# Strassen's scheme for the feed-forward up projection of a two-layer encoder

## The chip, the cores and the metric

The kernel runs on one core of a Trainium2 chip. The metric is the device time of one execution in microseconds (us); less is better. TensorE (PE in the profile) multiplies matrices, VectorE (DVE), ScalarE (ACT) and GpSimd (POOL) do element-wise work, and SyncE (SP) issues the transfers.

## The reference

Two layers over 512 tokens of 1024 features, in float32. The part that the change touches is the end of each layer:

```python
x = x + merged @ w_out[l]                       # 512x1024 @ 1024x1024
h = rms_norm(x, norm_ffn[l])                    # x * rsqrt(mean(x*x) + eps) * g
x = x + jnp.square(jax.nn.relu(h @ w_ff1[l])) @ w_ff2[l]   # 1024x4096, 4096x1024
```

Ahead of it each layer projects `x`, runs three kinds of attention, and sums their gated branches into `merged`; none of that is changed.

## The kernel before

Everything is feature-major: a tile is 128 features by 512 tokens, so `x` is eight tiles `x[0..7]`, and a result tile of a projection is one PSUM bank. For precision every operand is split into a high part that TensorE takes as it is and the rest: weights into `whi` (a copy on ACT, L140) and `wlo = raw - whi` (a subtraction on DVE, L142), inputs likewise. A product is three matmuls, `whi*xgh`, `whi*xgl` and `wlo*xgh` (`feature_tile`, L326, matmul at L333). `Stream.take` (L127) loads 512 KB of weights (eight 128x128 blocks) into one of three `raw` buffers and splits them.

`merge` (L907) ends with the output projection: eight tiles of 8 x 3 matmuls over 512 tokens. As each ends, DVE adds it to `x[m]` (L935) and `norm_part` (L264) makes the feed-forward's input: `xgh` on ACT (L273), `xgl` on DVE (L274), the square of `x[m]` on ACT (L284), added into `acc` on POOL (L285). The input is not yet divided by the root mean square: that factor, one per token, is found meanwhile and multiplied on afterwards.

`ffn` (L946) follows. **Up**: 32 tiles `up(f)` of 8 x 3 matmuls over 512 tokens; the first four are interleaved so that `norm_sums` (L296: eight small matmuls `ps_sum` over `acc`, then a chain on DVE) and `norm_rows` (L317: the factor spread to all partitions, `rb`) fall between them. What leaves PSUM is `max(ps, 0) * rb` (DVE, L957), its square split into `ah` (ACT) and `al` (DVE, L961 and L962). **Down**: after every 16 up tiles, eight tiles over the 16 new features, each added to `x[m]` by DVE (L991).

TensorE runs its matmuls in the order in which they are written. The queues of the other engines are ordered by a scheduler: what a `high_priority` block encloses (all of a weight's load and split) is taken ahead of its place, by `ahead` = 30 steps. An engine works its queue strictly in order. Buffers: `raw`, `whi`, `wlo` three each, `xgh` and `xgl` eight each; PSUM banks `mm` three, `s` two, `pt` two, `y` one.

## Time and profile before

| | |
|---|---|
| median of 3 runs | 1852.36 us (1851.02 to 1852.7) |
| profiled execution, its own time | 1852.28 us |
| its span in the profile | 1850.4 us |
| granted TensorE clock over the span | 0.993 |
| busy share: PE, DVE, ACT, POOL | 98%, 54%, 42%, 18% |

The span runs from the first to the last recorded instruction; the time has 1.9 us around it. A duration is that of one instruction by itself; instructions in a queue overlap a little, so the distance from start to start in a row of them is shorter.

### The profile page before, as it was taken

What the parts mean: (1) busy time and instruction counts of PE and PEld (TensorE: products, weight loads), DVE (VectorE), ACT (ScalarE), POOL (GpSimd) and SP (SyncE); (2) the same over time, 40 slices, a digit from 0 to 9 for tenths busy, and PEclk for the clock granted to TensorE, in tenths of its full rate; (3) what the DMA queues carried; (4) which work ended last, traced back from release to release, by engine and by line L of the source; (5) the groups of instructions that cost most, each with busy time, mean ns of one, the idle gap of its engine ahead of it and who ended that gap; (6) DMA issues with size and microseconds to landing.
All of it is one profiled execution on the core that took longest, in us unless ns stands there. A gap on an engine that the chain in (4) does not pass through costs nothing.

```text
span 1850.4 us, 23224 instructions
## 1 busy us (share of the span) xinstructions
PE 1811.2 (98%) x8496; PEld 1492.8 (81%) x8496; DVE 995.2 (54%) x1894; ACT 783.1 (42%) x1369; POOL 332.6 (18%) x307
## 2 busy tenths in 40 slices
...
GB/s 180 153 168 115 102 177 153 117 97 81 114 171 91 94 100 91 95 99 109 115 118 149 154 110 112 176 149 120 84 89 135 150 91 92 102 92 93 101 114 57
DMA packets 84225, 217.84 MB, mean 118 GB/s; under 512 B 13696, under 2 KB 16768, under 8 KB 84112
## 3 DMA queue, kind: packets, MB, share of 16 engines
...
## 4 chain that ended last, share of the span: by engine, by line
PE 85%; DVE 6%; ACT 3%; DMA 2%; issue 2%; POOL 1%; SPq 1%; ACTq 0%; DVEq 0%; POOLq 0%
PE ps L333 38%; PE ps_t L368 15%; PE ps_f L333 14%; PE ps_o L333 5%; PE ps_b L803 4%; PE ps_s L683 3%; PE ps_y L726 3%; PE ps_p L713 2%; DMA qq<-nat 1%; PE ps_q L585 1%; POOL wlo L142 1%; SPq L600 1%; DVE wlo L142 1%; ACT whi L140 1%; DVE pr L692 0%
## 5 line engine op out<-in xcount | busy, mean ns | idle before, releaser
L140 ACT ACTIVATE whi<-raw 128x1024 fp32r<-128x1024 f32 (+1 forms) x337 | 307.4, 919 | 772.0 <-issue 318.1
L142 DVE TENSOR_TENSOR wlo<-raw,whi 128x1024 fp32r<-128x1024 f32 (+2 forms) x237 | 287.1, 1212 | 233.7 <-ACT whi L140 233.1
L333 PE MATMUL ps<-ah,wlo 128*128 128x512 f32 x512 | 201.7, 394 | 0.0
L333 PE MATMUL ps<-ah,whi 128*128 128x512 f32 x512 | 201.7, 394 | 0.0
L333 PE MATMUL ps<-al,whi 128*128 128x512 f32 x512 | 201.7, 394 | 0.0
L333 PE MATMUL ps<-xgh,whi 128*128 128x512 f32 x512 | 199.4, 390 | 0.0
L333 PE MATMUL ps<-xgh,wlo 128*128 128x512 f32 x512 | 199.2, 389 | 0.0
L333 PE MATMUL ps<-xgl,whi 128*128 128x512 f32 x512 | 199.2, 389 | 0.0
L333 PE MATMUL ps_f<-xgh,whi 128*128 128x512 f32 x464 | 197.2, 425 | 0.0
L333 PE MATMUL ps_f<-xgl,whi 128*128 128x512 f32 x464 | 183.3, 395 | 0.0
L333 PE MATMUL ps_f<-xgh,wlo 128*128 128x512 f32 x464 | 183.2, 395 | 0.0
L142 POOL TENSOR_TENSOR wlo<-raw,whi 128x1024 fp32r<-128x1024 f32 x50 | 120.8, 2416 | 222.2 <-ACT whi L140 178.2
L368 PE MATMUL ps_t<-whi,xgh 128*128 128x512 f32 x384 | 151.4, 394 | 6.8 <-ACT whi L140 6.8
L368 PE MATMUL ps_t<-wlo,xgh 128*128 128x512 f32 x384 | 150.2, 391 | 0.0
L368 PE MATMUL ps_t<-whi,xgl 128*128 128x512 f32 x384 | 150.2, 391 | 0.0
L285 POOL TENSOR_TENSOR acc<-acc,t 128x512 f32<-128x512 f32 x24 | 41.5, 1730 | 499.1 <-ACT t L284 489.7
L716 DVE TENSOR_TENSOR ptl<-ps_p,pth 128x512 fp32r<-128x512 f32 x144 | 85.8, 600 | 67.8 <-ACT pth L715 66.9
L333 PEld LDWEIGHTS ps<-ah,wlo 128*128 128x128 f32 x512 | 95.7, 187 | 23.8
L333 PEld LDWEIGHTS ps<-ah,whi 128*128 128x128 f32 x512 | 95.7, 187 | 23.8
L333 PEld LDWEIGHTS ps<-al,whi 128*128 128x128 f32 x512 | 95.7, 187 | 23.5
L333 PEld LDWEIGHTS ps<-xgh,wlo 128*128 128x128 f32 x512 | 96.1, 188 | 20.2
L333 PEld LDWEIGHTS ps<-xgl,whi 128*128 128x128 f32 x512 | 96.1, 188 | 19.9
...
## 6 DMA issues: line engine op xcount, KB each, us to landing
...
```

Of the source, the lines that this page charges most:

```text
L140: nc.scalar.activation(out=hi[:, c : c + v], in_=raw[:, c : c + v], func=AF.Copy)
L142: k.lo_engine.tensor_tensor(out=lo[:, c : c + w], in0=raw[:, c : c + w], in1=hi[:, c : c + w].bitcast(F32), op=ALU.subtract)
L285: (engine or nc.gpsimd).tensor_tensor(out=self.acc, in0=self.acc, in1=sq, op=ALU.add)
L333: nc.tensor.matmul(out=ps, lhsT=a[:, k], rhs=b[k], start=first and k == 0 and j == 0, stop=last and k == n - 1 and j == 2)
L368: nc.tensor.matmul(out=pss[t][:, 0:width], lhsT=a[k][:, t * P : t * P + P], rhs=b[:, i], start=c == 0 and i == 0 and j == 0, stop=last and ...
L585: nc.tensor.transpose(ps[0:rows, t * P : (t + 1) * P], src(t), self.ident)
L600: nc.sync.dma_start(out=s[rows, u].bitcast(F32), in_=x[own].bitcast(F32))
L683: nc.tensor.matmul(out=ps[:, 0:n], lhsT=a[:, i * P : (i + 1) * P], rhs=b[:, 0:n], start=j == 0, stop=j == len(terms) - 1)
L713: nc.tensor.transpose(ps[:, o + (i - kb) * P : o + (i - kb + 1) * P], pr[:, offs[i] + kb * P : offs[i] + (kb + 1) * P], self.ident)
L716: nc.vector.tensor_tensor(out=pl[:, 0:w], in0=ps[:, 0:w], in1=ph[:, 0:w].bitcast(F32), op=ALU.subtract)
L726: nc.tensor.matmul(out=yps[:, kb * P : T], lhsT=qkv[2][kb // 2][:, kb % 2, h, :], rhs=head[h][gi][x][:, o : o + T - kb * P], start=gi == 0 ...
L803: nc.tensor.matmul(out=pss[u], lhsT=chunk[a][:, u, k], rhs=y[b][k], start=k == 0 and j == 0, stop=k == 3 and j == 2)
```

## The change

A pair of up tiles (256 features by 512 tokens, 1024 deep) is computed as 2x2 blocks by Strassen's scheme in Winograd's form: seven products of half depth, half features and half tokens in place of eight. Of the inputs (halves of the depth times halves of the tokens) and of the weights, four sums or differences each enter beside the plain blocks, and the seven results are summed into the four blocks of the pair.

- Weights (`Stream.take_pair`): two loads of 512 KB, four subtractions of 512 columns on POOL (`tw`), and four splits instead of two: `bh`/`bl` (512 columns), `whi`/`wlo`, and twice `twh`/`twl` (1024 each); two buffers each for `bh`, `bl`, `tw`, `twh`, `twl`.
- Inputs (`norm_pair`, in the place of `norm_split`): the tiles `x[m]` and `x[m + 4]` together give the seven factors as `xgh`/`xgl` and `sh`/`sl`. It is called as the output projection's tiles end, whose order is now 0, 4, 1, 5, 2, 6, 3, 7. `sh` and `sl` lie in a pool on the side on which the last branch's buffers were.
- Products (`pair_products`): 16 pairs of 7 x 4 x 3 = 84 matmuls over 256 tokens, in four PSUM banks, alternately `y, mm, mm, mm` and `s, s, pt, pt`. The first pair runs depth block by depth block, the others product by product.
- Sums (`pair_sum`): a copy of 256 columns on ACT, then four additions on DVE into `z` (one buffer), the later of them reading what the earlier wrote. Relu, square and `ah` follow on ACT over 1024 columns, `al` on DVE. The factor `rb` no longer multiplies here.
- `down` runs after every four pairs, over 8 features' tiles at a time; its result is multiplied by `rb*rb` on DVE and then added to `x[m]`, two instructions for one.
- `norm_sums` is written behind pair 1 and `norm_rows` behind pair 2.

The new layout of `w_ff1` (blocks of a pair side by side) is left out of this diff.

```diff
@@ class Stream @@
+    def take_pair(self, pool, *key):
+        k, nc = self.k, self.k.nc
+        raw = [k.pw.tile([P, 1024], F32, tag="raw", name="raw") for _ in range(2)]
+        sums = [pool.tile([P, 1024], F32, tag="tw", name="tw", bufs=2) for _ in range(2)]
+        w = {}
+        def split(names, src, n, tags):
+            hi, lo = (p.tile([P, n], F32R, tag=t, name=t, **b) for p, t, b in tags)
+            nc.scalar.activation(out=hi[:, 0:n], in_=src[:, 0:n], func=AF.Copy)
+            nc.vector.tensor_tensor(out=lo[:, 0:n], in0=src[:, 0:n], in1=hi[:, 0:n].bitcast(F32), op=ALU.subtract)
+            for i, name in enumerate(names):
+                w[name] = tuple(x[:, 512 * i : 512 * i + 512].rearrange("p (k m) -> p k m", m=P) for x in (hi, lo))
+        with k.tc.high_priority(k.ahead):
+            for i in range(2):
+                nc.sync.dma_start(out=raw[i], in_=self.ap[self.layer, :, self.at + 1024 * i : self.at + 1024 * i + 1024])
+            b = [raw[i][:, 512 * j : 512 * j + 512] for i in range(2) for j in range(2)]
+            t = [sums[i][:, 512 * j : 512 * j + 512] for i in range(2) for j in range(2)]
+            sub = lambda out, x, y: nc.gpsimd.tensor_tensor(out=out, in0=x, in1=y, op=ALU.subtract)
+            plain = ((k.pw, "whi", {}), (k.pw, "wlo", {}))
+            summed = ((pool, "twh", dict(bufs=2)), (pool, "twl", dict(bufs=2)))
+            split(["b11"], raw[0], 512, ((pool, "bh", dict(bufs=2)), (pool, "bl", dict(bufs=2))))
+            split(["b21", "b22"], raw[1], 1024, plain)
+            sub(t[0], b[1], b[0])
+            sub(t[1], b[3], t[0])
+            split(["t1", "t2"], sums[0], 1024, summed)
+            sub(t[2], b[3], b[1])
+            sub(t[3], b[2], t[1])
+            split(["t3", "t4"], sums[1], 1024, summed)
...
@@ class Kern @@
+    def norm_pair(self, l, vcol, pool, kt, x):
+        nc = self.nc
+        h2 = T // 2
+        a, b = slice(0, h2), slice(h2, T)
+        g = self.gain(l, vcol + kt)
+        if kt < 4:
+            self.half = self.half if kt else {}
+            t = self.half[kt] = self.tmp()
+            nc.scalar.activation(out=t, in_=x, func=AF.Copy, scale=g)
+            return
+        t = self.half.pop(kt - 4)
+        q = pool.tile([P, 3, h2], F32, tag="sq", name="sq", bufs=1)
+        sub = lambda out, u, v: nc.vector.tensor_tensor(out=out, in0=u, in1=v, op=ALU.subtract)
+        h = self.px.tile([P, T], F32R, tag="xgh", name="xgh")
+        lo = self.px.tile([P, T], F32R, tag="xgl", name="xgl")
+        nc.scalar.activation(out=h, in_=x, func=AF.Copy, scale=g)
+        sub(q[:, 1], t[:, a], t[:, b])
+        nc.vector.scalar_tensor_tensor(out=t[:, b], in0=x[:, b], scalar=g, in1=t[:, b], op0=ALU.mult, op1=ALU.add)
+        sub(q[:, 0], t[:, b], t[:, a])
+        nc.vector.scalar_tensor_tensor(out=q[:, 2], in0=x[:, a], scalar=g, in1=q[:, 0], op0=ALU.mult, op1=ALU.subtract)
+        nc.vector.scalar_tensor_tensor(out=lo, in0=x, scalar=g, in1=h.bitcast(F32), op0=ALU.mult, op1=ALU.subtract)
+        f = {"a12": [y[:, a] for y in (h, lo)], "a22": [y[:, b] for y in (h, lo)]}
+        h = self.px.tile([P, T], F32R, tag="xgh", name="xgh")
+        lo = self.px.tile([P, T], F32R, tag="xgl", name="xgl")
+        nc.scalar.activation(out=h, in_=t, func=AF.Copy)
+        sub(lo, t, h.bitcast(F32))
+        f |= {"a11": [y[:, a] for y in (h, lo)], "s1": [y[:, b] for y in (h, lo)]}
+        h = pool.tile([P, 3, h2], F32R, tag="sh", name="sh", bufs=4)
+        lo = pool.tile([P, 3, h2], F32R, tag="sl", name="sl", bufs=4)
+        nc.scalar.activation(out=h, in_=q, func=AF.Copy)
+        sub(lo, q, h.bitcast(F32))
+        for i in range(3):
+            f[f"s{2 + i}"] = [y[:, i] for y in (h, lo)]
+        self.xf.append(f)
...
-    def norm_rows(self):
-        nc = self.nc
-        ps = self.pt.tile([P, T], F32, tag="pt", name="ps_r")
+    def norm_rows(self, tag=None):
+        nc = self.nc
+        ps = self.bank(tag, "ps_r") if tag else self.pt.tile([P, T], F32, tag="pt", name="ps_r")
...
@@ merge @@
-                self.norm_part(l, V_FFN, m, x[m])
-            outs = [out(m) for m in range(KT)]
+                self.norm_pair(l, V_FFN, pool, m, x[m])
+                self.norm_square(m, x[m])
+            self.xf = []
+            outs = [out(m) for m in (0, 4, 1, 5, 2, 6, 3, 7)]
...
+    PRODUCTS = (
+        ("b11", "a11", 0, 0),
+        ("b21", "a12", 1, 0),
+        ("t2", "s2", 1, 1),
+        ("t3", "s3", 2, 0),
+        ("t1", "s1", 2, 1),
+        ("t4", "a22", 3, 0),
+        ("b22", "s4", 3, 1),
+    )
+    def pair_products(self, w, tags, steps):
+        nc = self.nc
+        h2 = T // 2
+        ps = [None] * 4
+        n = len(self.xf)
+        for i, k in steps:
+            stationary, moving, bank, half = self.PRODUCTS[i]
+            if ps[bank] is None:
+                ps[bank] = self.bank(tags[bank], f"ps_w{bank}")
+            out = ps[bank][:, half * h2 : half * h2 + h2]
+            hi, lo = w[stationary]
+            xh, xl = self.xf[k][moving]
+            for j, (a, b) in enumerate(((hi, xh), (hi, xl), (lo, xh))):
+                nc.tensor.matmul(out=out, lhsT=a[:, k], rhs=b, start=k == 0 and j == 0 and i in (0, 1, 3, 5), stop=k == n - 1 and j == 2 and i in (0, 2, 4, 6))
+            yield
+        self.ps = ps
+    def pair_sum(self, ps, z):
+        nc = self.nc
+        h2 = T // 2
+        add = lambda out, x, y: nc.vector.tensor_tensor(out=out, in0=x, in1=y, op=ALU.add)
+        two = lambda x: x.rearrange("p (u t) -> p u t", u=2)
+        p1 = self.tmp()[:, 0:h2]
+        nc.scalar.activation(out=p1, in_=ps[0][:, 0:h2], func=AF.Copy)
+        add(z[:, 0:5:4], two(ps[1]), p1.unsqueeze(1).to_broadcast([P, 2, h2]))
+        add(z[:, 5:7], two(ps[2]), z[:, 4].unsqueeze(1).to_broadcast([P, 2, h2]))
+        add(z[:, 3], ps[2][:, h2:T], z[:, 5])
+        add(z[:, 1:3], two(ps[3]), z[:, 5:7])
+        return z[:, 0:4].rearrange("p (u v) t -> p u (v t)", u=2)
...
@@ ffn @@
-            pa = self.pool(ctx, "act", 16)
-            xg = self.nx
-            def up(f, out):
-                hi, lo = self.streams[l].take(1024, "f1", f)
-                ps = self.bank("s" if f == 3 else "mm", "ps_1")
-                yield from self.feature_tile(ps, [c.rearrange("p (k m) -> p k m", m=P) for c in (hi, lo)], *xg)
+            pf = self.pool(ctx, "ffn", 1)
+            pa = self.pool(ctx, "act", 4)
+            take = lambda j: self.streams[l].take_pair(pf, "f1", j)
+            def up(j, w, a):
+                steps = [(i, k) for k in range(4) for i in range(7)] if j == 0 else [(i, k) for i in range(7) for k in range(4)]
+                yield from self.pair_products(w, (("y", "mm", "mm", "mm"), ("s", "s", "pt", "pt"))[j % 2], steps)
+                c = self.pair_sum(self.ps, pf.tile([P, 7, T // 2], F32, tag="z", name="z"))
+                nc.scalar.activation(out=c, in_=c, func=AF.Relu)
+                nc.scalar.activation(out=c, in_=c, func=AF.Square)
+                h, lo = pa.tile([P, 2, T], F32R, tag="ah", name="ah"), pa.tile([P, 2, T], F32R, tag="al", name="al")
+                nc.scalar.activation(out=h, in_=c, func=AF.Copy)
+                nc.vector.tensor_tensor(out=lo, in0=c, in1=h.bitcast(F32), op=ALU.subtract)
+                for u in range(2):
+                    a[0].append(h[:, u])
+                    a[1].append(lo[:, u])
+            def down(q, m, a):
+                ps = self.mm.tile([P, T], F32, tag="mm", name="ps_2")
+                w = self.streams[l].take(1024, "f2", 8 * q, m)
+                yield from self.feature_tile(ps, [c.rearrange("p (k m) -> p k m", m=P) for c in w], *a)
                 t = self.tmp()
-                nc.vector.scalar_tensor_tensor(out=t, in0=ps, scalar=0.0, in1=self.rb, op0=ALU.max, op1=ALU.mult)
-                h = pa.tile([P, T], F32R, tag="ah", name="ah")
-                lo = pa.tile([P, T], F32R, tag="al", name="al")
-                nc.scalar.activation(out=h, in_=t, func=AF.Square)
-                nc.vector.tensor_tensor(out=t, in0=t, in1=t, op=ALU.mult)
-                nc.vector.tensor_tensor(out=lo, in0=t, in1=h.bitcast(F32), op=ALU.subtract)
-                out[0].append(h)
-                out[1].append(lo)
-            for half in range(2):
+                nc.vector.tensor_tensor(out=t, in0=ps, in1=rb2, op=ALU.mult)
+                nc.vector.tensor_tensor(out=x[m], in0=x[m], in1=t, op=ALU.add)
+                if q == 3:
+                    if l + 1 < DEPTH:
+                        nc.sync.dma_start(out=self.xd[:, m], in_=x[m])
+                        self.norm_part(l + 1, V_MIX, m, x[m])
+                    else:
+                        nc.sync.dma_start(out=self.a["out"][:, m], in_=x[m])
+            w = take(0)
+            for q in range(4):
                 a = ([], [])
-                ups = [up(16 * half + f, a) for f in range(16)]
-                if half == 0:
-                    for u in ups[0:2]:
-                        for _ in range(7):
-                            next(u)
-                    self.norm_sums()
-                    next(ups[0])
-                    next(ups[1])
-                    for _ in range(7):
-                        next(ups[2])
-                    self.norm_rows()
-                    next(ups[2])
-                    for _ in range(7):
-                        next(ups[3])
-                for u in ups:
-                    run_all(u)
-                if half == 1 and l + 1 < DEPTH:
+                for j in range(4 * q, 4 * q + 4):
+                    ahead = take(j + 1) if j % 4 < 3 else None
+                    run_all(up(j, w, a))
+                    w = ahead
+                    if j == 1:
+                        self.norm_sums()
+                    if j == 2:
+                        self.norm_rows("mm")
+                        rb2 = self.rb
+                        nc.vector.tensor_tensor(out=rb2, in0=rb2, in1=rb2, op=ALU.mult)
+                if q == 3 and l + 1 < DEPTH:
                     self.norm_begin()
-                for m in range(KT):
-                    ps = self.mm.tile([P, T], F32, tag="mm", name="ps_2")
-                    for c in range(2):
-                        hi, lo = self.streams[l].take(1024, "f2", 16 * half + 8 * c, m)
-                        run_all(self.feature_tile(ps, [w.rearrange("p (k m) -> p k m", m=P) for w in (hi, lo)], a[0][8 * c : 8 * c + 8], a[1][8 * c : 8 * c + 8], first=c == 0, last=c == 1))
-                    nc.vector.tensor_tensor(out=x[m], in0=x[m], in1=ps, op=ALU.add)
-                    if half == 1:
-                        if l + 1 < DEPTH:
-                            nc.sync.dma_start(out=self.xd[:, m], in_=x[m])
-                            self.norm_part(l + 1, V_MIX, m, x[m])
-                        else:
-                            nc.sync.dma_start(out=self.a["out"][:, m], in_=x[m])
+                downs = [down(q, m, a) for m in range(KT)]
+                for d in downs[0:2]:
+                    for _ in range(6):
+                        next(d)
+                for i, d in enumerate(downs):
+                    if i == 5 and q < 3:
+                        w = take(4 * q + 4)
+                    run_all(d)
...
@@ run @@
-                self.merge(l, y, x)
+                ps = self.pool(xctx, "sums", 1, side="right")
+                self.merge(l, y, x, ps)
```

On DVE, at the end of the output projection (`ps_o` are its results; `x_5224` is the last tile of `x`, `nv` reads the sums of squares), before:

```order
L935 TENSOR_TENSOR x_5224<-x_5224,ps_o 128x512
L142 TENSOR_TENSOR wlo<-raw,whi 128x1024
L274 SCALAR_TENSOR_TENSOR xgl<-x_5224,vec,xgh 128x512
L304 TENSOR_SCALAR nv<-ps_sum 128x4
```

and now (`t_5729` is the scaled `x[3]`, `sq` the three sums of inputs):

```order
L1008 TENSOR_TENSOR x_5224<-x_5224,ps_o 128x512
L139 TENSOR_TENSOR bl<-raw,bh 128x512 x2
L333 SCALAR_TENSOR_TENSOR t_5729<-x_5224,vec,t_5729 128x256
L336 SCALAR_TENSOR_TENSOR xgl<-x_5224,vec,xgh 128x512
L139 TENSOR_TENSOR twl<-tw,twh 128x1024 x2
L328 TENSOR_TENSOR sq<-t_5729 128x256
L328 TENSOR_TENSOR xgl<-t_5729,xgh 128x512
L139 TENSOR_TENSOR wlo<-raw,whi 128x1024
L335 SCALAR_TENSOR_TENSOR sq<-x_5224,vec,sq 128x256
L328 TENSOR_TENSOR sl<-sq,sh 128x768
```

The rests `bl` and `twl` of the first pair's weights stand behind the last addition of the output projection, and the last input factors `sl` behind them and behind a `wlo` of the second pair.

On DVE, from the first pair's sums (`ps_w_58..` are its PSUM banks, `ps_w_5986` to `ps_w_6036` those of the second pair) to the reader of the sums of squares, now:

```order
L1055 TENSOR_TENSOR z<-ps_w_5864,z 128x512
L139 TENSOR_TENSOR bl<-raw,bh 128x512
L1082 TENSOR_TENSOR al<-z,ah 128x1024
L139 TENSOR_TENSOR wlo<-raw,whi 128x1024
L139 TENSOR_TENSOR twl<-tw,twh 128x1024 x2
L1055 TENSOR_TENSOR z<-ps_w_5986,t_6062 128x2x256
L178 TENSOR_TENSOR wlo<-raw,whi 128x1024
L1055 TENSOR_TENSOR z<-ps_w_6011,z 128x512
L1055 TENSOR_TENSOR z<-ps_w_6011,z 128x256
L1055 TENSOR_TENSOR z<-ps_w_6036,z 128x512
L377 TENSOR_SCALAR nv<-ps_sum 128x4
```

The matmuls `ps_sum` take the PSUM bank `ps_w_6011`, so they wait for its last reader, `z<-ps_w_6011,z 128x256`. A `wlo` of pair 3's weights, the two `twl` of pair 2's and a `wlo` of the down projection now stand ahead of it in the queue (pairs are counted from 0).

On POOL, at the end of the output projection (`t_57..` are squares of `x[m]`), before:

```order
L285 TENSOR_TENSOR acc<-acc,t_5658 128x512
L285 TENSOR_TENSOR acc<-acc,t_5697 128x512
L285 TENSOR_TENSOR acc<-acc,t_5736 128x512
L285 TENSOR_TENSOR acc<-acc,t_7632 128x512
```

and now:

```order
L358 TENSOR_TENSOR acc<-acc,t_5694 128x512
L358 TENSOR_TENSOR acc<-acc,t_5731 128x512
L148 TENSOR_TENSOR tw<-raw 128x512 x2
L148 TENSOR_TENSOR tw<-raw,tw 128x512 x2
L148 TENSOR_TENSOR tw<-raw 128x512
L148 TENSOR_TENSOR tw<-raw,tw 128x512
L358 TENSOR_TENSOR acc<-acc,t_5783 128x512
L148 TENSOR_TENSOR tw<-raw 128x512
L148 TENSOR_TENSOR tw<-raw,tw 128x512
```

The four subtractions for pair 0 stand behind the `acc` of the seventh tile in the output projection's order (`t_5731`, of `x[3]`), followed by two of pair 1's; only then comes the last `acc`.

## Rows read from the trace of the kernel before

**Rows 1.** The page's busy line: busy us, share of the span, instructions.
```profile
PE 1811.2 (98%) x8496; PEld 1492.8 (81%) x8496; DVE 995.2 (54%) x1894; ACT 783.1 (42%) x1369; POOL 332.6 (18%) x307
```

**Rows 2.** The page's chain that ended last, shares of the span by engine.
```profile
PE 85%; DVE 6%; ACT 3%; DMA 2%; issue 2%; POOL 1%; SPq 1%; ACTq 0%; DVEq 0%; POOLq 0%
```

**Rows 3.** The chain's pieces at layer 0's up projection: start, length, what.
```profile
571.42 9.55 PE ps L333 x42
580.97 0.79 PE ps_sum L293 x8
...
588.61 337.69 PE ps L333 x1467
```

**Rows 4.** Windows, output projection and half up: PE, PEld, DVE, ACT, POOL busy, clock, DMA, GB/s.
```profile
526.62:571.42 44.80, 44.80 (x194) 36.10 (x193) 23.19 (x28) 17.55 (x25) 10.31 (x6) 1.00 0.33 98
571.42:749.00 177.58, 177.58 (x777) 144.57 (x776) 79.91 (x111) 43.88 (x51) 1.79 (x1) 1.00 0.32 95
```

**Rows 5.** Timeline of PE, attention of layer 0: start, us, instruction.
```profile
446.27 0.28 PE L726 MATMUL ps_y<-pth,v 128*128 128x256 f32 x1
446.39 0.28 PE L726 MATMUL ps_y<-ptl,v 128*128 128x256 f32 x1
```

**Rows 6.** The same view, earlier.
```profile
423.36 0.52 PE L683 MATMUL ps_s<-st 96*128 96x256 f32 x3
423.71 0.60 PE L585 MATMUL ps_q<-ident,tok 128*96 128x128 f32 x4
424.07 0.48 PE L333 MATMUL ps_f<-xgh,whi 128*128 128x512 f32 x1
```

**Rows 7.** Groups of DVE by form: busy us, mean ns; idle before.
```profile
L142 DVE TENSOR_TENSOR wlo<-raw,whi 128x1024 fp32r<-128x1024 f32 x227 | 279.7, 1232 | 226.6 <-ACT whi L140 225.9 <-DMA t<-rows 0.5
...
L991 DVE TENSOR_TENSOR x<-x,ps 128x512 f32<-128x512 f32 x32 | 22.0, 688 | 119.0 <-PE ps L333 119.0
L716 DVE TENSOR_TENSOR ptl<-ps_p,pth 128x256 fp32r<-128x256 f32 x48 | 20.3, 422 | 30.4 <-ACT pth L715 29.7
```

**Rows 8.** Groups of ACT by form.
```profile
L140 ACT ACTIVATE whi<-raw 128x1024 fp32r<-128x1024 f32 x227 | 240.4, 1061 | 725.8 <-issue 315.5 <-PE ps L333 246.7 <-PE ps_t L368 96.0
L140 ACT ACTIVATE whi<-raw 128x512 fp32r<-128x512 f32 x102 | 61.5, 621 | 25.1 <-PE ps_t L368 20.4 <-issue 2.7 <-PE ps_f L333 2.1
```

**Rows 9.** Timeline of POOL, two additions of one form.
```profile
356.06 1.28 POOL L812 TENSOR_TENSOR mg<-mg,cb 128x512 f32<-128x512 f32 x1 [27.20 <-DVE cb L811]
...
396.12 2.27 POOL L812 TENSOR_TENSOR mg<-mg,cb 128x512 f32<-128x512 f32 x1 [0.70 <-DVE rs_y L252]
```

**Rows 10.** Timeline of DVE beside the second of them.
```profile
396.04 1.21 DVE L142 TENSOR_TENSOR wlo<-raw,whi 128x1024 fp32r<-128x1024 f32 x1
397.17 1.25 DVE L254 TENSOR_TENSOR rs_t<-rs_y 128x4 f32<-128x4 f32 x1
...
398.85 0.16 DVE L254 TENSOR_TENSOR rs_t<-rs_y 128x4 f32<-128x4 f32 x1
```

**Rows 11.** Timeline of SP's queue, one weight load.
```profile
602.40 0.33 SPq L137 DMA_DIRECT2D raw<-w  x1
```

**Rows 12.** Windows behind that issue, columns as in rows 4.
```profile
603.36:605.60 2.24, 2.24 (x12) 1.85 (x11) 0.35 (x1) 0.10 (x1) 0.00 (x0) 1.00 0.77 227
605.60:607.80 2.20, 2.20 (x12) 1.81 (x11) 1.90 (x3) 1.48 (x2) 0.00 (x0) 1.00 0.02 7
```

**Rows 13.** Windows around two idle stretches of PE.
```profile
130.90:133.60 2.70, 0.00 (x0) 0.00 (x0) 1.29 (x4) 0.30 (x1) 1.04 (x1) 0.94 1.00 222
133.60:136.70 3.10, 3.05 (x8) 2.47 (x9) 1.38 (x3) 1.60 (x5) 0.54 (x2) 0.50 0.92 206
...
1049.30:1052.60 3.30, 0.00 (x0) 0.00 (x0) 1.26 (x4) 0.27 (x1) 1.00 (x1) 0.82 1.02 225
1052.70:1058.30 5.60, 5.60 (x16) 4.53 (x17) 1.48 (x4) 2.26 (x7) 1.73 (x2) 0.50 0.71 187
```

**Rows 14.** Timeline of DVE at the output projection's end.
```profile
571.46 0.69 DVE L935 TENSOR_TENSOR x<-x,ps_o 128x512 f32<-128x512 f32 x1 [2.80 <-PE ps_o L333]
```

10 lines of the change are left out of this document (7 added, 3 removed).

## The prediction

> **What bounds the kernel now.** I read the page's busy line first: TensorE is busy 98% of the span, DVE 54%, ACT 42%, POOL 18% [rows 1]. The chain that ended last says the same, 85% of it is PE [rows 2]. Then the chain's pieces at the stage that is changed: from the end of the output projection at 571.42 us PE runs 42 matmuls of 512 columns, the eight small `ps_sum`, and soon one stretch of 1467 matmuls, through up and down projections, without a stop [rows 3]. So up is bound by TensorE alone, at 337.69/1467 = 0.2302 us a matmul, and the 768 of a layer cost 176.8 us; the window over half of it shows DVE at 79.91 and ACT at 43.88 of 177.58 us, POOL at 1.79 [rows 4]. Anything that takes columns from PE here gains, until another engine comes too late.
>
> **What is removed and added on TensorE.** 32 x 8 x 3 = 768 matmuls of 512 columns become 16 x 7 x 4 x 3 = 1344 of 256, each with its own weights. The trace has 256-column matmuls in short rows: two start 0.12 us apart [rows 5]; three end (423.71 - 423.36)/3 = 0.117 us apart [rows 6]. I take 0.117: 1344 x 0.117 = 157.2 us, so **19.6 us gained per layer**. With 0.12 it would be 15.5. The down projection keeps its 768 matmuls, and the loads stay 64 of 512 KB per layer, so SP's queue and the bytes do not change. No stretch of 256-column matmuls here is longer than three, so a sustained pace is not shown; it is a rival below.
>
> **Durations for the rest.** DVE: 1024 columns 1.23 us, 512 columns 0.69, 256 columns 0.42 [rows 7]. ACT: 1024 columns 1.06, 512 columns 0.62 [rows 8]. POOL, 512 columns: 1.28 alone, but 2.27 where it meets a DVE instruction with two operands in SBUF [rows 9]. In that meeting DVE's `wlo` ran to the full, and a tiny DVE instruction behind it took 1.25 us, 0.16 otherwise, while POOL finished [rows 10]. So the two exclude each other, and take turns: an estimate for one turn is the sum, 1.28 + 1.2. I price each POOL subtraction at 1.28 plus its turns; the bounds are 1.28 and 2.27. A weight load of 512 KB is issued at 602.40 and moves until about 605.6 [rows 11, 12]: 3.2 us, 3.5 with its semaphore (my estimate).
>
> **In the steady state** a pair takes PE 84 x 0.117 = 9.83 us. DVE has three rests and `al` of 1024 columns, `bl` and three sums of 512, one of 256: 4 x 1.23 + 4 x 0.69 + 0.42 = 8.1. ACT has three splits of 1024, one of 512, one copy, relu, square and `ah`: 6 x 1.06 + 0.62 + 0.37 = 7.4 (the 0.37 an estimate from half of the 512's, and more). POOL has 5.1. Each fits. But what excludes POOL on DVE (the rests, `al`) is 5.6, with POOL's 5.1 it is 10.7, over 9.83. Four pairs fall 3.5 us behind; the eight down tiles after them (8 x 24 x 0.2302 = 44.2 us) make it good. So each quarter costs little, and the loss lies where the pipeline is empty: **at the start of up**. `norm_pair` itself adds some 10 us of DVE work to an output projection in which DVE is busy 23.19 of 44.80 [rows 4]; that stays hidden.
>
> **Start of up** (time 0: the end of the output projection's last matmul). The rests `bl` and `twl` of pair 0 stand in DVE's queue behind the last addition to `x[7]`, which starts 0.04 us after that matmul [rows 14] and ends at 0.7. POOL's four subtractions stand behind the `acc` of `x[3]`, about -3.3 to -2.0, and run from -2.0 to 3.8, with DVE's `bl` between. Then DVE: second `bl` 4.4, two of `norm_pair` 5.4, `twl` 6.6 and 7.7. Pair 0 runs block by block: its third product needs the first `twl` at 0.94 and gets it at 6.6; the fourth gets its own at 7.7. Block 0 ends at 8.95 in place of 21 x 0.117 = 2.46. Blocks 1 and 2 follow till 13.9; block 3 needs the last `sl`, behind five DVE instructions (0.35 + 0.65 + 1.22 + 0.35 + 0.92, the 768 columns between the rows), four POOL turns of 1.28, a copy on ACT of 0.8 and the handovers: 7.7 + 3.5 + 5.1 + 0.8 + 0.4 = 17.5. Pair 0 ends at 19.25 in place of 9.83: **9.4 lost**. Without the exclusion it is 4.6, my lower bound: the same queue orders, but POOL ends at 3.2, and ACT and DVE follow at 5.5.
>
> **Pair 1.** Its first `twl` is ready 4.6 us after pair 0's end, needed after 26 x 0.117 = 3.04: **1.6 lost** (1.2 to 2.7).
>
> **Sums of squares.** `norm_sums` comes behind pair 1, and `ps_sum` takes a bank that is free once DVE has added up pair 1. Ahead of that addition in DVE's queue stand pair 3's `wlo` and pair 2's two `twl`, ahead of those `twl` in ACT's queue pair 3's `whi`. That needs its load, which needs a `raw` buffer, which three POOL subtractions of pair 2 free, and these need a `tw` buffer, free after pair 1's last `twl` (19.25 + 5.7 = 25). In turns with DVE they end at 29.4; load to 33.0; `whi` 34.05; two `twh` 36.0; `wlo`, `twl`, `twl` on DVE, the last at 37.55; then the first addition 38.15, a down `wlo` in turn with POOL 39.95, the second and the third addition, which frees the bank, 40.95. PE has ended pair 1 at 19.25 + 1.6 + 9.83 = 30.7: **10.3 lost**. In the light case 8.1, since the load is in it either way.
>
> **Later quarters** refill the same pipeline, but beside down tiles; I leave 1.2 us for each of three, an estimate of one 1024-column rest by which a refill is late: **3.6** (0 to 10). **Clock**: after idle stretches of 2.7 and 3.3 us the granted clock was 0.50 for 3.1 and 5.6 us [rows 13], so half of these is lost, 1.6 to 2.8 us. Of two such stops per layer not all of that counts, since PE waits for others anyway: **2.2** (0 to 5.6).
>
> **Sum per layer**: lost 9.4 + 1.6 + 10.3 + 3.6 + 2.2 = 27.1, gained 19.6, so 7.5 slower; both layers' queues stand alike: 15.0. The end adds one DVE instruction behind the last matmul, 0.6. Against the profiled run's 1852.28 (the median is 1852.36): 1852.28 + 15.6 = **1867.9 us**.
>
> **Rivals.**
> A, other side: the side chain is lighter. If DVE and POOL hardly hinder each other and the clock holds, the losses are 4.6 + 1.2 + 8.1 + 1.5 = 15.4, below 19.6, and the time is 1852.28 - 2 x 4.2 + 0.6 = 1844.5; with everything covered 1852.28 - 39.2 + 0.6 = 1813.7. It decides when a layer loses under 19.6. For it speaks that POOL alone takes 1.28 and the loads find a queue that is idle; against it the queue order, by which the weights' rests begin only at the last addition whatever the prices are.
> B, no difference: both nearly balance, about 1852.
> C: a 256-column matmul in a long row costs more than half of a 512-column one, since each brings its own weights. Four of 128 columns start (424.07 - 423.71)/4 = 0.09 us apart [rows 6], more than a quarter of 0.2302; halfway by columns 256 would cost 0.09 + 0.1402/3 = 0.137, and 1344 of them 184 us: 7 us more than before in place of 19.6 less. Some of the waits would be covered; with 20 left, 1852.28 + 2 x 27 + 0.6 = 1907. The three at 0.117 speak against it, also in front of such a row.
> The Trainium skill, "TensorE: Matmul & The Clock Gate", section "Back-to-back issue gap", gives sustained spacings of about 81 ns for 128 columns and 131 for 512; read in between, 256 columns are some 98 ns, 0.745 of a 512-column one (my estimate), which would make up 1344 x 0.2302 x 0.745 = 231 us, 54 more a layer. By its formula for an isolated matmul, N/2.4 + 2.5, the change would save 19.0 us a layer. The trace agrees with the formula: no 512-column matmul here comes at 131 ns, they come at 230.
> D: more waits, above 1886: a stop at every quarter as at the first.
> That the change doesn't do what it says is excluded, since the order of PE's queue has 84 matmuls of 256 columns for each pair.
>
> **How the numbers follow.** The forecast has 0.55, A 0.26, B 0.13, C 0.03, D 0.03. A measurement of this kernel can tell about 0.2%, 3.7 us. Faster by more: 0.26; within: 0.13, B; slower: 0.61. The range: low the light case, 1844. High: per layer 9.4 + 1.6 + 10.3 = 21.3 lost at the start, 5.6 by the clock, 10 in the quarters, 36.9 less 19.6, gives 1852.28 + 34.6 + 0.6 = 1887.5; I take 1886.
>
> **What the changed profile would show.** PE idle in the first microseconds of up, released by DVE `twl`, then by `sl`; a stop of about 10 us before `ps_sum`, released by DVE `z`, with ACT's `whi` waiting for a load ahead of it; a granted clock of 0.5 behind both; rows of 256 columns at 0.117 apart; up and down otherwise without stops; in each layer a time some 7 us longer from the output projection's end to the layer's end. The prediction is wrong if the pace differs from 0.117 or if there is no stop at `ps_sum`.

## The result, and the profile after

The changed kernel takes 1878.58 us (median of 4 runs, 1874.08 to 1882.04), the kernel before, run beside it, 1851.97 (4 runs, 1851.02 to 1852.70): ratio 1.0138, 95% interval 1.0125 to 1.0151. It is 26.6 us slower; 15.6 slower was forecast, so the size was off by 11 us, within the stated range (1844 to 1886). The profiled execution took 1877.65 us, with a span of 1875.9 and a granted clock of 0.982.

The page of the changed kernel, busy line and chain by engine (against [rows 1, 2]):

```profile
PE 1794.6 (96%) x9648; PEld 1535.2 (82%) x9648; DVE 1184.2 (63%) x2064; ACT 918.9 (49%) x1513; POOL 539.4 (29%) x435
...
PE 49%; DVE 6%; issue 4%; POOL 3%; ACT 3%; DMA 2%; SPq 1%; DVEq 0%; ACTq 0%; POOLq 0%
```

PE is busy 16.6 us less than before, and yet the program is 25 us longer: time went from PE's work into waits. POOL is busy 206.8 us more, DVE 189.0.

The chain that ended last, from layer 0's start of up (start, length, what), against [rows 3]:

```profile
599.26 2.18 POOL tw L148
...
604.45 1.24 DMA raw<-w
...
611.61 2.16 POOL tw L148
...
613.83 2.15 POOL tw L148
...
616.04 1.84 PE ps_sum L366 x8
617.88 12.04 PE ps_w L1047 x84
...
630.39 9.94 PE ps_w L1047 x84
640.33 44.80 PE ps L406 x192
```

Where there was one row of 1467 matmuls without a stop, the chain now goes through POOL's subtractions and a weight load before it reaches `ps_sum`. The pair of 84 behind it takes 12.04 us, the next 9.94.

Windows (columns as in rows 4): pairs 0 and 1; the stop and `ps_sum`; pairs 2 and 3; the first down projection; pairs 4 to 7; and the two stretches at half clock (a granted clock of 0.50, the level of 1.2 GHz).

```profile
575.24:606.10 30.86, 23.93 (x169) 22.64 (x167) 24.62 (x22) 13.50 (x17) 20.20 (x13) 0.83 0.25 72
606.10:617.80 11.70, 1.88 (x11) 1.78 (x9) 8.02 (x9) 5.08 (x6) 6.12 (x4) 0.62 0.23 81
617.80:640.17 22.37, 22.37 (x172) 22.28 (x171) 14.63 (x35) 9.38 (x11) 0.67 (x1) 0.90 0.29 94
640.17:684.97 44.80, 44.80 (x195) 36.17 (x193) 28.73 (x28) 14.77 (x16) 12.72 (x8) 1.00 0.39 118
684.97:725.88 40.91, 39.92 (x338) 39.52 (x336) 27.95 (x30) 21.67 (x25) 13.47 (x8) 1.00 0.25 78
578.10:588.30 10.20, 6.68 (x28) 5.98 (x28) 10.20 (x8) 4.10 (x5) 7.83 (x6) 0.50 0.34 104
608.80:622.50 13.70, 6.46 (x30) 6.49 (x31) 11.52 (x31) 6.67 (x8) 6.79 (x4) 0.50 0.30 96
```

From the output projection's end to the layer's end, layer 0 took 926.30 - 571.42 = 354.9 us before and 942.23 - 575.24 = 367.0 now: 12.1 more. Layer 1 has 12.0 more, the end 1.1. (The output projection of layer 0 ends 3.8 later, and layer 1 ahead of its up projection is 3.6 shorter; these cancel. e1 has the same program up to there, and its output projection ends at 571.4, as in the kernel before, so the 3.8 are not of this change.) So nearly all lies in up. Its first quarter takes 30.86 + 11.70 + 22.37 = 64.9 us, a later one 40.91.

Timeline of PE, with what it waited for in brackets:

```profile
577.47 0.38 PE L1047 MATMUL ps_w<-xgh,bl 128*128 128x256 f32 x1 [1.84 <-DVE bl L139]
...
579.72 0.58 PE L1047 MATMUL ps_w<-sh,twh 128*128 128x256 f32 x1 [1.50 <-ACT twh L138]
...
582.40 0.58 PE L1047 MATMUL ps_w<-sh,twl 128*128 128x256 f32 x1 [1.89 <-DVE twl L139]
...
592.73 0.28 PE L1047 MATMUL ps_w<-sl,twh 128*128 128x256 f32 x1
...
594.36 0.28 PE L1047 MATMUL ps_w<-xgh,bh 128*128 128x256 f32 x1
...
599.18 0.38 PE L1047 MATMUL ps_w<-sh,twl 128*128 128x256 f32 x1 [1.58 <-DVE twl L139]
...
616.04 1.84 PE L366 MATMUL ps_sum<-ones,acc 128*128 128x2 f32 x8 [9.82 <-POOL tw L148]
```

Three stops of 1.5 to 1.9 us open pair 0, one of 1.58 falls in pair 1, and one of 9.82 stands before `ps_sum`. The name POOL `tw` there is the event that came last; what held `ps_sum` shows on DVE's timeline:

```profile
576.05 3.08 DVE L139 TENSOR_TENSOR bl<-raw,bh 128x512 fp32r<-128x512 f32 x2
...
581.13 2.35 DVE L139 TENSOR_TENSOR twl<-tw,twh 128x1024 fp32r<-128x1024 f32 x2
...
591.21 1.06 DVE L328 TENSOR_TENSOR sl<-sq,sh 128x768 fp32r<-128x768 f32 x1 [0.91 <-ACT sh L345]
...
609.11 1.23 DVE L139 TENSOR_TENSOR wlo<-raw,whi 128x1024 fp32r<-128x1024 f32 x1 [2.34 <-ACT whi L138]
610.25 2.36 DVE L139 TENSOR_TENSOR twl<-tw,twh 128x1024 fp32r<-128x1024 f32 x2
612.52 0.68 DVE L1055 TENSOR_TENSOR z<-ps_w,t 128x512 f32<-128x512 f32 x1
613.12 1.72 DVE L178 TENSOR_TENSOR wlo<-raw,whi 128x1024 fp32r<-128x1024 f32 x1
614.76 1.73 DVE L1055 TENSOR_TENSOR z<-ps_w,z 128x512 f32<-128x512 f32 x3
```

The first sum of pair 1 runs at 612.52, though PE ended that pair at 606.1: a `wlo` and two `twl` stand ahead of it. And that `wlo` waits for ACT's `whi`, which waits for a load:

```profile
608.02 1.06 ACT L138 ACTIVATE whi<-raw 128x1024 fp32r<-128x1024 f32 x1 [3.54 <-DMA raw<-w]
```

POOL's two forms of subtraction (groups by form: count, busy, mean ns):

```profile
L148 POOL TENSOR_TENSOR tw<-raw,tw 128x512 f32<-128x512 f32 x64 | 109.3, 1708 | 65.3 <-DMA raw<-w 63.8
L148 POOL TENSOR_TENSOR tw<-raw 128x512 f32<-128x512 f32 x64 | 104.6, 1635 | 343.6 <-DMA raw<-w 166.2 <-DVE twl L139 87.9 <-issue 71.3
```

They take 1.64 and 1.71 us on the mean, between the 1.28 alone and the 2.27 beside DVE [rows 9].

### The profile page after: what moved, and what is told of

Same layout as the page of the kernel before. It is cut to its first block, busy times and chain, and to the rows that moved or that the text cites. A ratio compares the mean times of both kernels' runs of the same rounds, so it can differ in the third digit from the quotient of the medians.

```text
span 1875.9 us, 26181 instructions
## 1 busy us (share of the span) xinstructions
PE 1794.6 (96%) x9648; PEld 1535.2 (82%) x9648; DVE 1184.2 (63%) x2064; ACT 918.9 (49%) x1513; POOL 539.4 (29%) x435
## 4 chain that ended last, share of the span: by engine, by line
PE 49%; DVE 6%; issue 4%; POOL 3%; ACT 3%; DMA 2%; SPq 1%; DVEq 0%; ACTq 0%; POOLq 0%
PE ps L406 19%; PE ps_w L1047 8%; PE ps_t L441 7%; PE ps_f L406 6%; POOL tw L148 3%; PE ps_o L406 2%; PE ps_b L876 2%; PE ps_s L756 1%; DVE z L1055 1%; PE ps_y L799 1%; DMA raw<-w 1%; PE ps_p L786 1%; DVE twl L139 1%; DMA qq<-nat 1%; POOL wlo L178 1%
## 5 line engine op out<-in xcount | busy, mean ns | idle before, releaser
L176 ACT ACTIVATE whi<-raw 128x1024 fp32r<-128x1024 f32 (+3 forms) x273 | 239.5, 885 | 358.4 <-PE ps_t L441 121.1
L178 DVE TENSOR_TENSOR wlo<-raw,whi 128x1024 fp32r<-128x1024 f32 (+3 forms) x173 | 216.8, 1253 | 87.9 <-ACT whi L176 87.8
L148 POOL TENSOR_TENSOR tw<-raw 128x512 f32<-128x512 f32 x64 | 104.6, 1635 | 343.6 <-DMA raw<-w 166.2
L148 POOL TENSOR_TENSOR tw<-raw,tw 128x512 f32<-128x512 f32 x64 | 109.3, 1708 | 65.3 <-DMA raw<-w 63.8
L138 ACT ACTIVATE twh<-tw 128x1024 fp32r<-128x1024 f32 x64 | 65.8, 1053 | 90.9 <-POOL tw L148 48.0
L1092 DVE TENSOR_TENSOR t<-ps,rb 128x512 f32<-128x512 f32 x64 | 44.1, 689 | 98.4 <-PE ps L406 98.4
L406 PEld LDWEIGHTS ps_f<-xgh,wlo 128*128 128x128 f32 x464 | 87.7, 189 | 20.0
L770 ACT ACTIVATE pr<-pr,mn 128x512 f32<-128x512 f32 (+3 forms) x128 | 71.5, 559 | 60.9 <-DVE mn L765 60.5
```

Source lines behind the costliest of these rows:

```text
L138: nc.scalar.activation(out=hi[:, 0:n], in_=src[:, 0:n], func=AF.Copy)
L148: sub = lambda out, x, y: nc.gpsimd.tensor_tensor(out=out, in0=x, in1=y, op=ALU.subtract)
L176: nc.scalar.activation(out=hi[:, c : c + v], in_=raw[:, c : c + v], func=AF.Copy)
L178: k.lo_engine.tensor_tensor(out=lo[:, c : c + w], in0=raw[:, c : c + w], in1=hi[:, c : c + w].bitcast(F32), op=ALU.subtract)
L406: nc.tensor.matmul(out=ps, lhsT=a[:, k], rhs=b[k], start=first and k == 0 and j == 0, stop=last and k == n - 1 and j == 2)
L770: nc.scalar.activation(out=p, in_=p, func=AF.Exp, bias=mn, scale=sign, accum_out=ls)
```

## The experiments

Two questions: is it really the late weights and the bank that cost the time, and what would it take to get the matmuls' gain. Each run is compared with the kernel before on the same chip.

| run | median us | before | ratio | 95% |
|---|---|---|---|---|
| e1_bank | 1877.80 | 1851.98 | 1.0135 | 1.0120 to 1.0150 |
| e2p_pool_order | 1876.10 | 1851.98 | 1.0126 | 1.0111 to 1.0141 |
| e2_start_order | 1870.12 | 1851.98 | 1.0096 | 1.0079 to 1.0112 |
| e3_both | 1868.88 | 1851.98 | 1.0088 | 1.0072 to 1.0103 |
| e5_sums_later | 1852.13 | 1852.60 | 0.9997 | 0.9988 to 1.0007 |
| e6_weights_first | 1849.25 | 1852.60 | 0.9980 | 0.9971 to 0.9990 |
| e7_summed_first | 1857.29 | 1852.60 | 1.0022 | 1.0013 to 1.0032 |
| e8_first_quarter | 1850.36 | 1853.50 | 0.9979 | 0.9970 to 0.9989 |
| e9_sums_alone | 1860.58 | 1853.50 | 1.0040 | 1.0027 to 1.0054 |
| e10_no_weight_sums | 1827.36 | 1851.85 | 0.9865 | 0.9848 to 0.9881 |
| e11_xg_right | 1867.42 | 1851.85 | 1.0084 | 1.0066 to 1.0102 |
| e12_sums_on_dve | 1854.84 | 1852.75 | 1.0008 | 1.0000 to 1.0017 |

In the diffs `behind(later, earlier)` is a new helper that only fixes the order of two instructions in one queue; `tail[i]` holds what the output projection's i-th tile issued (0: the addition to `x`, 1: POOL's `acc`, 2: the square, 3: the first scaled copy), `last_sub`, `last_rest` and `last_high` the last subtraction, rest and high part of pair 0's weights.

### The stop before `ps_sum`

**e1_bank**: another bank for `ps_sum`.

```diff
-        ps = self.pt.tile([P, T], F32, tag="pt", name="ps_sum")
+        ps = self.bank(tag, "ps_sum")
...
-                        self.norm_sums()
+                        self.norm_sums("mm")
```

> The sums of squares go into a bank of group mm, which pair 0 has left, instead of one of pair 1's; the matmuls and every other instruction stay. Theory (three waits, each with its own cause): the stop of 9.8 us before ps_sum goes, and with it the half clock behind it; what is late next is pair 2's second twl, for a stop of 1 to 3 us, and a small one at pair 3; 8 to 11 us less per layer, 1857 to 1863 us. Rival 1 (the stop is the weights' chain, not the bank; it only moves to pair 2 and pair 3): 1873 us or more. Rival 2 (POOL and DVE excluding each other is what costs, wherever the wait shows): 1873 us or more too.

Measured 1877.80: no gain, as both rivals had it; the time alone does not tell them apart. The stop did not go, it moved behind pair 2, to `ps_r`, the next thing that PE needs of this chain. Timeline of PE in e1:

```profile
623.44 1.19 PE L394 MATMUL ps_r<-dg,onesr 128*128 128x512 f32 x2 [8.73 <-DVE z L1055]
```

and of DVE between:

```profile
607.53 0.16 DVE L377 TENSOR_SCALAR nv<-ps_sum 128x4 f32<-128x4 f32 x1
...
608.73 1.28 DVE L288 TENSOR_SCALAR rs_y<-nv 128x4 int32<-128x4 int32 x1
...
611.31 1.21 DVE L178 TENSOR_TENSOR wlo<-raw,whi 128x1024 fp32r<-128x1024 f32 x1
612.44 1.26 DVE L291 SCALAR_TENSOR_TENSOR rs_t<-rs_t,nv 128x4 f32<-128x4 f32 x1
...
618.01 0.86 DVE L388 TENSOR_SCALAR dg<-ident,rl 128x128 fp32r<-128x128 f32 x4
...
622.61 0.68 DVE L1055 TENSOR_TENSOR z<-ps_w,t 128x512 f32<-128x512 f32 x1
```

`nv` now runs at 607.5 instead of 617.9, but its chain shares DVE with the same `twl`, `wlo` and `z`, and instructions over four columns take 1.26 to 1.28 us there, 0.16 where POOL is quiet (the row of `nv`). `dg`, which `ps_r` reads, is ready only at 618.9, and `ps_r` still waits, since it takes the first `mm` bank of pair 2, which that pair's first sum reads at 622.6. In the changed kernel the same sum runs at 624.4, while PE is still busy with pair 2. So the first bank was one of two causes in a row; the second is a late DVE, which holds the factor and the next bank.

**e9_sums_alone**: the changed kernel, with both steps one pair later.

```diff
-                    if j == 1:
-                        self.norm_sums()
                     if j == 2:
+                        self.norm_sums()
+                    if j == 3:
                         self.norm_rows("mm")
```

> The changed kernel with nothing but ps_sum one pair later (behind pair 2) and ps_r one pair later (behind pair 3); all queues at the start of up as in the change. Theory (the stop at ps_sum and the start are separate, and e1_bank failed only because ps_r then waited for the same chain on DVE): the stop of 9.8 us and the half clock behind it go, as between e3_both and e5_sums_later (16.8 us): 1860 to 1866 us. Rival (the start's delay and the sums' share one chain, and only both together help): 1870 us or more.

Measured 1860.58, as the theory had it: some 18 us less than the changed kernel. By ratios it is 1.0138 - 1.0040 = 0.98%, 18.1 us, over two layers 9.1 each: the stop of 9.82 is gone. PE in e9:

```profile
618.55 0.95 PE L366 MATMUL ps_sum<-ones,acc 128*128 128x2 f32 x8
```

Not all of it is gained: pair 2 now stops for `twh` and `twl` (0.81 and 0.95) and, with what the clock takes there, is 3.9 us longer than a pair without stops.

### The start of up

**e2p_pool_order**: POOL takes pair 0's four subtractions ahead of the `acc` of `x[3]` and `x[7]`.

```diff
+            for _, acc in self.tail[6:8]:
+                self.behind(acc, self.last_sub)
```

> On POOL alone the additions of the squares of x[3] and x[7] are queued behind the four subtractions for pair 0's weights; DVE's order stays. Theory (DVE's queue order sets most of the start): the subtractions start some 6 us earlier, at about 7 us before the output projection's end, and meet DVE less; but bl and twl still stand behind the last addition to x: pair 0 loses 5 to 6 us in place of 9.4, 3 to 7 us less per layer, 1865 to 1872 us; the stop before ps_sum stays at 9 to 10 us. Rival (POOL is the cause of the start's loss, by lateness and exclusion): the whole 9.4 goes, 1860 us or less.

Measured 1876.10: both missed, a gain of 2.5 at most, with intervals that overlap. The rests stayed where they were, behind the last addition to `x`. Pair 0 ends 16.7 us after the output projection instead of 19.1, but pair 1 takes 15.0 instead of 11.7, with stops of 0.95 and 2.02 for `twh` and `twl`: what pair 0 gained, pair 1 lost.

**e2_start_order**: that addition too goes behind pair 0's rests.

```diff
+            self.behind(self.tail[7][0], self.last_rest)
```

> As e2p_pool_order, and on DVE the last addition to x is queued behind pair 0's bl and twl. Theory: pair 0 loses 0.6 to 3.5 us in place of 9.4, pair 1 about none, the stop before ps_sum stays at 8 to 10 us: 8 to 10 us less per layer, 1858 to 1863 us. Rival (exclusion, the same work in another order): pair 0 still loses over 6 us, since the last input factors come later by what the weights come earlier; 1870 us or more.

Measured 1870.12, a gain of 0.42%, 8 us: less than the theory had it, and at the rival's edge. Timeline of PE and, below, the window of the stretch at half clock in e2:

```profile
574.37 0.39 PE L1050 MATMUL ps_w<-xgh,bh 128*128 128x256 f32 x1 [0.98 <-ACT bh L138]
...
575.75 0.38 PE L1050 MATMUL ps_w<-xgh,bl 128*128 128x256 f32 x1 [0.88 <-DVE bl L139]
...
577.49 0.58 PE L1050 MATMUL ps_w<-sh,twl 128*128 128x256 f32 x1 [0.77 <-DVE twl L139]
```

```profile
576.70:583.50 6.80, 5.91 (x27) 5.59 (x27) 6.33 (x6) 2.75 (x5) 5.85 (x4) 0.50 0.47 157
```

The stops are now below 1 us each, but the granted clock fell to 0.50 for 6.8 us all the same. Pairs 0 and 1 take 27.1 instead of 30.9 us from the output projection's end, pair 1 without a stop. Pair 0 still loses 7.5 us, and not by the clock alone: the last `xgl` and `sl` are ready at 587.4 and 588.7, and PE, late as it is, still stops for them (0.17 and 0.29). Without the half clock it would have come to them earlier and waited longer, so the rival named the cause: the last input factors come later by what the weights come earlier. The stop at `ps_sum` is still 9.3: it has a cause of its own.

**e3_both** is e2 with e1's bank:

```diff
-                        self.norm_sums()
+                        self.norm_sums("mm")
```

> e1_bank and e2_start_order together. Theory: the two waits have separate causes, so the gains add up, 16 to 20 us per layer: 1839 to 1847 us, less than the kernel before (1852). Rival (one chain of weights sets both): the gains don't add up, 1855 us or more.

Measured 1868.88, within the noise of e2: a stop of 8.66 us stands at `ps_r`, as in e1. The time is the rival's, but e1 shows why the gains don't add up: there was none to add.

**e5_sums_later** is e2 with e9's edit (`ps_sum` behind pair 2, `ps_r` behind pair 3); against e3:

```diff
-                    if j == 1:
-                        self.norm_sums("mm")
                     if j == 2:
+                        self.norm_sums("pt")
+                    if j == 3:
```

> On top of e3_both: ps_sum one pair later (behind pair 2, in a bank of pt), ps_r one pair later (behind pair 3). In e1_bank and e3_both the stop of 9 us had moved to ps_r, which waits for the eight dg on DVE; these end the chain from nv, which is mixed with pair 1's sums and a wlo. Theory (the chain from ps_sum to ps_r takes DVE about 12 us there, and PE had only one pair, 9.9 us, to cover it, begun too late): with a pair's time more nothing waits for it; the stop goes but for 0 to 2 us, and the half clock behind it: 8 to 10 us less per layer than e3_both (1868.9), 1848 to 1854 us. Rival (DVE as a whole is over its capacity in the first quarter, so that any wait removed comes back at the next reader of DVE: pair 3's twl, or the first ah of down): 1862 us or more.

Measured 1852.13, ratio 0.9997: no difference from the kernel before. The order at the start is worth 1.0040 - 0.9997 = 0.43%, 8 us, beside e9's 18; together they are the whole 26.6. The gain of the matmuls is still missing, so about as much as they give is still lost elsewhere.

### Where the gain stays

**e6_weights_first**: more of the last tiles' work (squares, `acc`, additions) behind pair 0's weights.

```diff
+            for e in self.tail[5:8]:
+                self.behind(e[1], self.last_sub)
+            for e in self.tail[6:8]:
+                self.behind(e[0], self.last_rest)
+                self.behind(e[2], self.last_high)
+            self.behind(self.tail[6][3], self.last_high)
```

> On top of e5_sums_later: all of pair 0's weights (bh, twh on ACT, the subtractions on POOL, bl and twl on DVE) are queued ahead of what follows from the seventh tile of the output projection instead of the eighth. Theory: the stops of 0.98 and 0.88 us at the first products, for bh and bl, go, and with them the 6.8 us at half clock that followed, 3.4 us; pairs 0 and 1 take about 21 us in place of 27.1: 5 to 6 us less per layer than e5_sums_later. Rival (the inputs of x[7] are then late: a stop at sl in the fourth depth block takes the place): 0 to 2 us less per layer, and the half clock comes a little later.

Measured 1849.25; the rival was right. Timeline of PE in e6: the weights are in time, and what follows from the last tiles is late. The second and third stop are for input factors. The first is for a PSUM bank: the fourth product takes the `mm` bank of the output projection's seventh tile, which is free when that tile is added to `x` (L1009), and the edit put this addition behind the weights.

```profile
575.17 0.35 PE L1050 MATMUL ps_w<-sh,twh 128*128 128x256 f32 x1 [1.20 <-DVE x L1009]
...
583.51 0.39 PE L1050 MATMUL ps_w<-xgh,bh 128*128 128x256 f32 x1 [1.74 <-ACT xgh L341]
...
585.32 0.39 PE L1050 MATMUL ps_w<-xgl,bh 128*128 128x256 f32 x1 [1.43 <-DVE xgl L329]
```

**e7_summed_first**: of each later pair's weights the plain split goes behind the summed ones of the pair before.

```diff
+            if key[1]:
+                k.behind(k.last_high, before[0])
+                k.behind(rest, before[1])
```

> On top of e6_weights_first, for all pairs: a pair's whi and wlo, which wait for its load, are queued behind twh and twl of the pair before. Theory: ACT stood waiting for that load with the pair before's twh behind it (2 to 3.5 us idle before whi); the stops of 0.7 to 0.85 us at twl in each later quarter go, and what is left of stops in the first: 2 to 4 us less per layer than e6_weights_first. Rival (these stops come from the POOL subtractions, which wait for a free tw, and not from the order): within 2 us in all of e6_weights_first.

Measured 1857.29: both missed. In the later quarters each pair 3 then waits 1.4 to 1.75 us for `twl`, and the first down projection 0.82 and 0.76 for `ah` and `al`.

**e8_first_quarter**: e6, and an order by hand for the splits of the first quarter (inputs of the last tiles, then pair 1 to 3).

```diff
+            self.behind(self.tail[5][0], rests[0])
+            for i in (2, 3):
+                self.behind(self.tail[5][i], highs[0])
...
+                    if j < 3:
+                        self.behind(self.highs[1], kept[-1][0])
+                        self.behind(self.rests[1], kept[-1][1])
```

> On top of e6_weights_first, in the first quarter alone: bh and bl of pair 0 ahead of what follows from the sixth tile, its twh and twl ahead of that tile's sh and sl; whi and wlo of pair 1 behind the last sh and sl, those of pairs 2 and 3 behind twh and twl of the pair before. Later quarters keep the order that e7_summed_first made worse. Theory (in e6 PE stops for twh 1.2 us, for the last tile's inputs 1.74 and 1.43 and for sl 0.83, with 6.8 us at half clock behind them; each stands in a queue behind work that is not yet needed): pairs 0 to 2 take 30 to 34 us in place of 38.6, 4 to 8 us less per layer, 1833 to 1841 us. Rival (DVE and POOL are full in these 20 us, so the order only chooses who waits): 1845 us or more.

Measured 1850.36. Pairs 0 to 2 took 34.4 us in place of 38.4 in e6, with one stop:

```profile
577.88 0.36 PE L1053 MATMUL ps_w<-sh,twh 128*128 128x256 f32 x1 [3.13 <-DVE x L1012]
```

Most of what was gained there went into stops of 0.81 at `ps_r` and 0.83 and 0.76 in the first down projection. The time is the rival's: each order tried chose who waits. But the stop of 3.13 is again for the seventh tile's bank, and it is this order that holds the bank, since the addition which frees it runs only at 577.06, behind the weights and the sixth tile's factors. Timeline of DVE:

```profile
577.06 1.27 DVE L1012 TENSOR_TENSOR x<-x,ps_o 128x512 f32<-128x512 f32 x2
```

A pair 0 in other banks was not tried; so the rival's reason, that DVE and POOL are full in these 20 us, is not shown.

**e10_no_weight_sums**: e6 without POOL's subtractions. It leaves the weights' sums out, so its result is another one; it shows only what they cost in time.

```diff
-            sub(t[0], b[1], b[0])
-            sub(t[1], b[3], t[0])
-            split(["t1", "t2"], sums[0], 1024, summed)
+            split(["t1", "t2"], raw[0], 1024, summed)
...
```

> e6_weights_first without the four POOL subtractions per pair: twh and twl are split from the loaded weights themselves, so the products with t1 to t4 use other weights (this part of the computation is left out); matmuls, splits and sums stay in number and size. Theory (what still costs in e6 is DVE and POOL getting in each other's way, and the longer chain from a load to twl): the two-SBUF instructions of DVE no longer wait, the stops of 0.5 to 0.9 us at twl in the later quarters go, those at the start shrink to 2 to 3 us per layer: 4 to 8 us less per layer than e6 (1849), 1833 to 1841 us. Rival (the rest of the loss is DVE's and ACT's own work, splits and sums of PSUM): 1845 us or more.

Measured 1827.36, faster than either expected: 0.9980 - 0.9865 = 1.15%, 21 us less than e6. Windows of e10, from just before up (573.2) into pair 2, and a later quarter:

```profile
572.00:600.00 28.00, 28.00 (x235) 27.73 (x235) 19.33 (x25) 15.50 (x21) 2.59 (x2) 1.00 0.24 76
...
662.65:701.99 39.34, 39.34 (x337) 39.34 (x336) 23.87 (x29) 21.66 (x25) 0.00 (x0) 1.00 0.36 107
```

PE runs through up without a stop at a clock of 1.00; what is left are two stops of 0.93 and 0.95 in the first down projection. So the weights' sums are what costs: 64 subtractions a layer, and the splits that wait for them. Whether by POOL's own time, by its turns with DVE, or by the longer way from a load to `twl`, this run does not say.

**e12_sums_on_dve**: the subtractions on DVE, where nothing takes turns with POOL's, with e5's later sums and a start of up ordered by hand, much as in e8.

```diff
-            sub = lambda out, x, y: nc.gpsimd.tensor_tensor(out=out, in0=x, in1=y, op=ALU.subtract)
+            sub = lambda out, x, y: nc.vector.tensor_tensor(out=out, in0=x, in1=y, op=ALU.subtract)
```

> The changed kernel with ps_sum and ps_r one pair later, the four subtractions of each pair on DVE in place of POOL, and at the start of up pair 0's weights queued ahead of what follows from the sixth tile of the output projection, pair 1's behind the last input factors. Theory (e10 shows that without the subtractions on POOL nothing stops in up; each holds DVE up for about 1.3 us where the two exclude each other): on DVE a subtraction costs 0.6 us and nothing waits for POOL; DVE then needs 8.1 + 2.4 = 10.5 us per pair, above the 9.9 of PE by little, which the down tiles make good; 5 to 9 us less per layer than e6_weights_first, 1831 to 1840 us. Rival (DVE is now over its capacity within a quarter and in-order, so that a subtraction waiting for a load holds up the sums of PSUM): stops of 1 to 3 us in each quarter, 1846 us or more.

Measured 1854.84, 1.0008: the rival was right. Up's later quarters run without stops, but the down projection now waits at each quarter's start for the last pair's squares, which stand at the end of DVE's and ACT's queues. Timeline of PE, and the window behind:

```profile
714.37 0.50 PE L410 MATMUL ps<-ah,whi 128*128 128x512 f32 x1 [0.99 <-ACT ah L1090]
...
715.63 0.80 PE L410 MATMUL ps<-al,whi 128*128 128x512 f32 x1 [0.76 <-DVE al L1091]
```

```profile
715.00:719.40 4.40, 3.77 (x10) 3.02 (x11) 1.77 (x3) 1.06 (x1) 0.00 (x0) 0.61 0.02 4
```

So POOL's exclusion is not the whole of it: moved to DVE, the same work comes out late somewhere else.

### The size of the gain

**e11_xg_right**: the kernel before, with up's inputs at the other end of SBUF.

```diff
-        self.px = self.pool(ctx, "xg", 8)
+        self.px = self.pool(ctx, "xg", 8, side="right")
```

> The kernel before with the eight xgh and eight xgl in the other end of SBUF, nothing else edited (all other tiles move down by 32 KB). In the trace of before a 512-column matmul of up takes 226.7 us per thousand, one of the output projection and of down 233.3, at the same clock. If the place of the moving operand sets that pace, up goes to about 0.233 us, 5 us per layer slower in up alone, 1858 us or more with the other uses of xgh; down may gain as its operands move down. Rival (it is set by the weights, the bank or what else runs): up stays at 0.2267, 1850 to 1855 us.

Measured 1867.42, 0.84% slower than before. Chain of waits in e11: the same pieces as in [rows 3], and a projection of layer 1's mixers that reads the same pool.

```profile
591.59 341.92 PE ps L333 x1467
...
961.31 31.56 PE ps_t L368 x135
```

A layer's down projection takes 4 x 44.80 us for 768 matmuls, in before, after and here. So up's share of the 1467, 1467 - 768 = 699, costs (341.92 - 179.2)/699 = 0.2328 us each here and (337.69 - 179.2)/699 = 0.2267 before. A window of before over the second half of up, 384 matmuls, gives 0.2267 directly:

```profile
749.48:836.53 87.05, 87.05 (x385) 72.07 (x384) 50.10 (x62) 24.76 (x31) 0.00 (x0) 1.00 0.32 97
```

The row of 135 took 30.84 before. Output and down projections, which read other pools, kept their pace. The place theory holds for what reads this pool; why a place is slower stays open. The pool of the moving operand alone does not set the pace either: in e10, over the 30 pairs that run product by product, matmuls of `sh`/`sl` come every 0.1135 us with `twh`/`twl` as weights and every 0.1197 with `whi`/`wlo` (other thirds of the same `sh` and `sl` tiles), and those of `xgh`/`xgl` with `twh`/`twl` every 0.1178. So the 0.117 is a mean of paces that differ by 5%; what sets them was not separated.

Of the versions that compute everything, e6 and e8 are the best: 0.2% below the kernel before, at the edge of what a measurement tells.

## Why the prediction was right

The sign was right, and for the reason given: DVE, POOL and one load cost more at the refill than the matmuls give back. e9 took away the stop at `ps_sum`, e2 a part of the start's loss, and with both, in e5, the kernel is as fast as before; e10 took the weights' sums away and most of the gain appeared. Step by step, from the output projection's end at 575.24:

| step | forecast | measured |
|---|---|---|
| last subtraction for pair 0 ends | 3.8 | 5.0 |
| second `twl` of pair 0 ends | 7.7 | 8.2 |
| last `sl` ends | 17.5 | 17.0 |
| pair 0 ends | 19.25 | 19.1 |
| stop in pair 1 | 1.6 | 1.58 |
| pair 1 ends | 30.7 | 30.9 |
| pair 3's `whi` begins | 33.0 | 32.8 |
| stop before `ps_sum` | 10.3 | 9.82 |
| lost in the first quarter, with the clock | 23.5 | 23.9 |
| lost in the later quarters | 3.6 | 4.6 |
| gained by the matmuls | 19.6 | 16.5 |
| a layer, net | 7.5 | 12.1 |
| the end | 0.6 | 1.1 |

(The first quarter's loss is 64.9 less four pairs of 9.85 and 1.6 for `ps_sum` and `ps_r`, which before has too; a later quarter loses 40.92 - 39.4 on the mean; 9.85 and 39.4 are what a pair and a quarter take in this kernel less their stops.)

**The term that was mis-sized** is the gain, "at 337.69/1467 = 0.2302 us a matmul, and the 768 of a layer cost 176.8 us". That row holds up and down projections, and 0.2302 is their mean: down runs at 44.80/192 = 0.2333, and what the change removes, up, at 0.2267, so 174.1 us. What was added is 4 x 39.4 = 157.6, very near the 157.2 forecast. The gain is 16.5, 3.1 less a layer, and these 6.2 us are most of the 9.8 by which the profiled run (25.4 us over before's) exceeds the forecast; the later quarters, the first one and the end make up the rest.

**Half clock** was priced at 2.2 a layer and cost about 3.6, within its bounds, although the stretches were 10.2 and 13.7 us, far longer than in [rows 13]. The first cost little: PE reached the first product with `sl` at 592.73, 0.5 us after `sl` was there, so it would have waited in any case. The second began in the stop itself: `ps_sum` took 1.7 us until the next matmul, 0.79 before [rows 3], and behind it 22.37 less two pairs of 9.85 and 0.47 for `ps_r`, 2.2, were lost.

**Right in size, incomplete in cause** was the step at `ps_sum`: it did wait for the bank, with the queue as told, but e1 shows that freeing the bank alone gains nothing. **Near in size by luck** were the later quarters: the forecast put 1.2 us on a late refill at each quarter's start; what came, 1.5, are stops for `twl` in its third and fourth pair (0.72 to 0.88 and 0.18 to 0.20). There the working had seen DVE and POOL fall behind, but counted it as made good by the down tiles.

**Rivals.** B, no difference, is out by the interval. C is out: a later quarter in e10 has 336 matmuls of 256 columns in 39.34 us, 0.1171 each, with their own weights every time. The Trainium skill's sustained spacings ("TensorE: Matmul & The Clock Gate", "Back-to-back issue gap"), by which, read in between as an estimate, the change would have lost 54 us a layer, don't describe these rows; its formula for an isolated matmul, 109 ns for 256 columns, is nearer to the 117 measured here, and still 7% below it. A did not come: POOL's subtractions take 1.64 and 1.71 us and not 1.28, the clock fell, and even e6 and e8, with queues ordered by hand, reached only 1849 and 1850. D did not come: later quarters lose 1.5 us each.
